# A two-layer encoder in float32: 36 of 44 gate-and-up tiles by seven half-size products in place of eight, the feed-forward in five groups

## The chip, the cores and the metric

The kernel runs on one core of one Trainium2 chip. The metric is the device time of one execution in microseconds (us), the median of several. The engines are named as in the profile: PE is TensorE (PEld its weight loads), DVE is VectorE, ACT is ScalarE, POOL is GpSimd, SP is SyncE, which here only issues transfers. A matmul of TensorE writes to PSUM (eight banks); DVE and ACT read from there.

## The reference, cut to what matters

Two layers on x of 512 positions by 1024 features, all in float32. Each layer mixes by attention and then runs a gated feed-forward, which is what the change is about:

```python
for l in range(DEPTH):                       # DEPTH = 2
    h = rms_norm(x, attn_norm_g[l])
    ...                                      # projections, retention, differential attention
    x = x + jnp.concatenate([ret, da], axis=-1) @ w_out[l]
    h = rms_norm(x, ffn_norm_g[l])
    x = x + (jax.nn.silu(h @ w_gate[l]) * (h @ w_up[l])) @ w_down[l]
```

w_gate and w_up are 1024 by 2816, w_down is 2816 by 1024.

## The kernel before, in words

**Three products for one.** A float32 matmul at full precision is made of three in the format fp32r: every operand is split into hi (the value rounded to fp32r) and lo (what is left), and a product is hi·hi + hi·lo + lo·hi (mm3, L184 to L187). For a piece of weights of 128 by 1024, SP loads it into a tile raw (three of these), ACT casts it to hi (L177), and DVE subtracts to get lo (L178); of hi and of lo there are three tiles each (NHL = 3). So ACT and DVE have to have prepared a piece before TensorE gets to it, and its hi and lo tiles come free only when TensorE has used them.

**The layout.** Features lie on the 128 partitions, positions (512) on the free axis. h2 is a list of eight pairs (hi, lo), one for each 128 features; the row factor 1/rms (rstd2) is put on after the product.

**The feed-forward (FFN, L637 onwards).** The 2816 inner features are 22 tiles of 128, in three groups: 8, 8 and 6. For each tile (loop over ff) come two chunks of weights, gate and up. Each is 8 times mm3, so 24 matmuls with 512 columns into a PSUM bank; DVE multiplies by rstd2 (L655, L658), ACT does SiLU on the gate (L105), DVE multiplies the two (L659), and split makes hi and lo of the result (L203 on ACT, L204 on DVE). After a group come the eight output pieces of "down" (loop over m): each loads 128 by 128·(tiles of the group) of w_down, runs mm3 over the group's tiles into one bank, and DVE adds it to x (residual, L614). After the last group of layer 0 the residual also makes the next layer's norm and split; after that of layer 1 it is stored.

**What sets the order.** The program text is one stream; the framework's scheduler then lays the instructions of each engine in an order of its own from planned times, and puts in semaphore waits. On the chip each engine runs its list strictly in that order, so an instruction that waits holds up all behind it on its engine. PSUM has two banks each of the tags acc, sc and o (any_bank goes round them) and two of aux.

**The start.** PE runs nine matmuls on a zeroed tile (L117) while the first data come. ACT issues the loads of the parameters (prm) and then of the first piece of x; SP issues the first weights in half pieces and the other pieces of x in turn.

Of the kernel before, what the change touches and what calls it, by code (L numbers as in the profile page):

```python
# [22 lines left out]
FT = DFF // P  # L23
EPS = 1e-6
C = 256
# [17 lines left out]

PRM_AG, PRM_FG, PRM_RG, PRM_QG, PRM_KG, PRM_DG = 0, 16, 32, 34, 36, 38
# [9 lines left out]
def encoder_kernel(ctx: ExitStack, tc: tile.TileContext, xT, wfirst, wsingle, wvv, wout, wgu, wdn, prm, lam, cst, outT):  # L54
    nc = tc.nc
# [3 lines left out]
    wpool = ctx.enter_context(tc.tile_pool(name="wpool", bufs=3))  # L59
# [25 lines left out]
    def any_bank():  # L85
        turn[0] += 1
        return (acc_bank, sc_bank, out_bank)[turn[0] % 3]()

    consts = {}

    def f32(ap):
        return ap.bitcast(F32)
# [15 lines left out]


    prm_sb = cpool.tile([P, PRM_N], F32, name="prm_sb")  # L110
    nc.scalar.dma_start(prm_sb, prm)

    warm = big("warm", F32R)
    nc.vector.memset(f32(warm), 0.0)
    warm_bank = aux_bank()
    for i in range(NWARM):
        nc.tensor.matmul(warm_bank, warm[:, :P], warm, start=True, stop=True)  # L117
# [44 lines left out]
    def load_chunk(src, n=1024, pieces=1):  # L162
# [2 lines left out]
            load_piece(new, src, i)  # L165
        return new

    def split_chunk(raw, n, pieces, first=False):
        hi = wpool.tile([P, 1024], F32R, tag="hi", name=nm("hi"), bufs=NHL)
        lo = wpool.tile([P, 1024], F32R, tag="lo", name=nm("lo"), bufs=NHL)  # L170
        q = n // pieces
        for i in range(pieces):
            s = slice(i * q, (i + 1) * q)
            if first and i == 0:
                nc.vector.tensor_copy(hi[:, s], raw[:, s])
            else:
                nc.scalar.copy(hi[:, s], raw[:, s])  # L177
            nc.vector.tensor_tensor(lo[:, s], raw[:, s], f32(hi[:, s]), op=ALU.subtract)  # L178
        return hi, lo

    def chunk(*a, **kw):
        return split_chunk(*load_chunk(*a, **kw))

    def mm3(out, L, R, start, stop):  # L184
        nc.tensor.matmul(out, L[0], R[0], start=start, stop=False)  # L185
        nc.tensor.matmul(out, L[0], R[1], start=False, stop=False)  # L186
        nc.tensor.matmul(out, L[1], R[0], start=False, stop=stop)  # L187

    def cut(pair, *idx):
        return tuple(t[idx] for t in pair)  # L190

    def split_scaled(src, col, tag, bufs):

        hi = big("hi", F32R, tag, bufs)
        lo = big("lo", F32R, tag, bufs)
        nc.scalar.activation(hi, src, AF.Copy, scale=col)  # L196
        nc.vector.scalar_tensor_tensor(lo, src, col, f32(hi), op0=ALU.mult, op1=ALU.subtract)
        return hi, lo

    def split(src, tag, bufs):  # L200
        hi = big("hi", F32R, tag, bufs)
        lo = big("lo", F32R, tag, bufs)
        nc.scalar.copy(hi, src)  # L203
        nc.vector.tensor_tensor(lo, src, f32(hi), op=ALU.subtract)  # L204
        return hi, lo
# [84 lines left out]
    def layer(l, n1, h, x_src, first_raw):  # L290
# [322 lines left out]
        def residual(m, xt, ps, n, hn, g):  # L613
            nc.vector.tensor_tensor(xt, xt, ps, op=ALU.add)  # L614
            if n is not None:
                n.add(xt)
                hn.append(split_scaled(xt, prm_sb[:, g + m : g + m + 1], "h", 16))

        def project_out(half, get, *then):
            parts = mix[4:] if half == 0 else mix[:4]  # L620
# [20 lines left out]

        rstd2 = n2.rows()
        n3, h3 = Norm(), []
        for a0, a1 in FFN:
            act = []
            for ff in range(a0, a1):
                pgu = []
                for gu in range(2):
                    w = [t.rearrange("p (k f) -> p k f", f=P) for t in chunk(wgu[l, ff, gu])]
                    ps = any_bank()  # L650
                    for kt in range(KT):
                        mm3(ps, cut(w, slice(None), kt), h2[kt], kt == 0, kt == KT - 1)
                    pgu.append(ps)
                g = big("g")
                nc.vector.tensor_tensor(g, pgu[0], rstd2, op=ALU.mult)  # L655
                func(g, g, AF.Silu)
                u = big("u")
                nc.vector.tensor_tensor(u, pgu[1], rstd2, op=ALU.mult)  # L658
                nc.vector.tensor_tensor(u, g, u, op=ALU.mult)  # L659
                act.append(split(u, *(("rn", 4) if ff - a0 < 2 and a0 else ("mix", NMIX))))  # L660
            last = a1 == FT
            for m in range(KT):
                w = chunk(wdn[l, m][:, a0 * P : a1 * P], (a1 - a0) * P)
                ps = any_bank()
# [12 lines left out]
    for kt in range(KT):  # L677
        if kt % 2 == 0:
            raws.append(new_chunk(1024, 2))
        load_piece(raws[-1], wfirst[0, kt // 2], kt % 2)  # L680
        xt = load_x(xT, kt, nc.scalar if kt == 0 else None)
        h.append(split_scaled(xt, prm_sb[:, PRM_AG + kt : PRM_AG + kt + 1], "h", 16))
        n.add(xt)
    for l in range(DEPTH):
        if l:
# [19 lines left out]
def _layout(inputs):  # L705
    import numpy as np

    f = {k: np.asarray(v) for k, v in inputs.items()}
    a = {}
    a["xT"] = f["x"].reshape(T, D).T.reshape(KT, P, T)  # L710
    w = f["w_in"].reshape(DEPTH, KT, P, 3584).transpose(0, 2, 1, 3)
    cols = {"rq": 0, "rk": 512, "rv": 1024, "rg": 1536, "dq": 2048, "dk": 2560, "dv": 3072}

    def sel(n, f, width):
        return w[:, :, :, cols[n] + f : cols[n] + f + width]

# [12 lines left out]
    g = f["w_gate"].reshape(DEPTH, KT, P, FT, P).transpose(0, 3, 2, 1, 4).reshape(DEPTH, FT, 1, P, 1024)  # L729
    u = f["w_up"].reshape(DEPTH, KT, P, FT, P).transpose(0, 3, 2, 1, 4).reshape(DEPTH, FT, 1, P, 1024)  # L730
    a["wgu"] = np.concatenate([g, u], 2)
# [43 lines left out]
```

## Time and profile before

| | |
|---|---|
| median of 3 runs | 1273.31 us (1273.26 to 1275.16) |
| the profiled execution | 1275.36 us |
| its span, first to last instruction | 1273.5 us |
| PE busy | 1264.8 us, 6201 matmuls |
| DVE / ACT busy | 769.7 / 569.8 us |
| read from HBM | 114.87 MB |
| granted TensorE clock, mean | 1.00 |

The profile gives an engine's busy time and, in groups by line and shape, the mean duration of an instruction. Matmuls overlap: one with 512 columns lasts 0.39 us, yet the next one starts long before it ends. So the time that a matmul costs is the distance from start to start, which the timeline shows, and not its duration. The same holds to a lesser degree for DVE and ACT.

### The profile page before, as it was taken

How to read it: one execution, taken by the hardware profiler on the slowest of the kernel's cores; microseconds unless marked ns; L12 is line 12 of the kernel's file. 1: busy time of each engine (PE TensorE's matmuls, PEld its weight loads, DVE VectorE, ACT ScalarE, POOL GpSimd, SP SyncE). 2: the span in 40 equal slices, each digit the busy share in tenths (PEclk: the TensorE clock that was granted, in tenths of full speed). 3: DMA queues.
4: the chain of work that ended last, by engine and by line, in shares of the span. 5: the costliest groups of instructions: out<-in, count | busy, mean ns of one | idle time of the engine just before them, and what ended most of it. 6: DMA issues, size and time to landing. Idle time of an engine off the chain costs nothing.

```text
span 1273.5 us, 15689 instructions
## 1 busy us (share of the span) xinstructions
PE 1264.8 (99%) x6201; PEld 1056.9 (83%) x6201; DVE 769.7 (60%) x1193; ACT 569.8 (45%) x886; POOL 17.3 (1%) x38
## 2 busy tenths in 40 slices
PE   9999999999999999999999999999999999999998
PEld 7888998778888888888888889987788888888887
DVE  6899759966443444344648997697754434443443
ACT  6777747554321322123438785564542223322221
POOL 1000000000000000000000000000000000000000
PEclk9999999999999999999999999999999999999999
DMA  7222224113333332322432122141233333333222
GB/s 266 83 67 67 67 66 133 58 60 114 90 97 96 99 99 84 115 91 81 159 117 83 50 84 66 51 149 51 66 116 99 99 91 93 98 99 99 99 76 91
DMA packets 36793, 120.07 MB, mean 94 GB/s; under 512 B 4208, under 2 KB 4208, under 8 KB 36592
## 3 DMA queue, kind: packets, MB, share of 16 engines
q1 hardware_dynamic: 36432, 118.77, 29.3%
q8 instruction: 48, 0.79, 0.2%
q10 hardware_dynamic: 288, 0.31, 0.1%
q14 instruction: 25, 0.20, 0.1%
HBM read 114.87 MB, written 4.19 MB: 93 GB/s over the span
## 4 chain that ended last, share of the span: by engine, by line
PE 97%; DVE 1%; ACT 1%; DMA 0%; issue 0%; SPq 0%
PE acc L185 15%; PE acc L186 15%; PE acc L187 15%; PE o L185 8%; PE o L187 8%; PE o L186 8%; PE sc L185 7%; PE sc L187 7%; PE sc L186 7%; PE sc L380 2%; PE o L481 1%; PE sc L465 1%; PE aux L396 1%; PE aux L137 1%; PE aux L136 1%; PE aux L441 1%
## 5 line engine op out<-in xcount | busy, mean ns | idle before, releaser
L177 ACT CAST hi<-raw 128x1024 fp32r<-128x1024 f32 (+2 forms) x211 | 215.0, 1021 | 511.8 <-issue 153.7
L185 PE MATMUL acc<-hi,hi 128*128 128x512 f32 (+1 forms) x914 | 337.6, 370 | 1.0 <-ACT hi L196 0.7
L186 PE MATMUL acc<-lo,hi 128*128 128x512 f32 (+1 forms) x914 | 337.8, 370 | 0.0
L187 PE MATMUL acc<-hi,lo 128*128 128x512 f32 (+1 forms) x914 | 337.1, 369 | 0.0
L178 DVE TENSOR_TENSOR lo<-raw,hi 128x1024 fp32r<-128x1024 f32 (+2 forms) x212 | 250.2, 1182 | 43.5 <-ACT hi L177 43.1
L185 PEld LDWEIGHTS acc<-hi,hi 128*128 128x128 f32 x914 | 172.4, 189 | 31.9 <-ACT hi L196 1.4
L186 PEld LDWEIGHTS acc<-lo,hi 128*128 128x128 f32 x914 | 172.6, 189 | 28.9 <-issue 1.2
L187 PEld LDWEIGHTS acc<-hi,lo 128*128 128x128 f32 x914 | 172.6, 189 | 28.0
L185 PE MATMUL o<-hi,hi 128*128 128x512 f32 (+1 forms) x438 | 163.9, 374 | 0.0
L186 PE MATMUL o<-lo,hi 128*128 128x512 f32 (+1 forms) x438 | 163.7, 374 | 0.0
L187 PE MATMUL o<-hi,lo 128*128 128x512 f32 (+1 forms) x438 | 163.6, 374 | 0.0
L185 PE MATMUL sc<-hi,hi 128*128 128x512 f32 x408 | 158.7, 391 | 0.3 <-ACT hi L177 0.3
L186 PE MATMUL sc<-lo,hi 128*128 128x512 f32 x408 | 159.0, 390 | 0.0
L187 PE MATMUL sc<-hi,lo 128*128 128x512 f32 x408 | 158.9, 389 | 0.0
L185 PEld LDWEIGHTS o<-hi,hi 128*128 128x128 f32 x438 | 82.4, 188 | 15.6 <-DVE sq L496 0.7
L186 PEld LDWEIGHTS o<-lo,hi 128*128 128x128 f32 x438 | 82.4, 188 | 14.8
L187 PEld LDWEIGHTS o<-hi,lo 128*128 128x128 f32 x438 | 82.4, 188 | 14.6
L185 PEld LDWEIGHTS sc<-hi,hi 128*128 128x128 f32 x408 | 76.9, 188 | 17.4 <-issue 0.8
L186 PEld LDWEIGHTS sc<-lo,hi 128*128 128x128 f32 x408 | 76.8, 188 | 16.1
L187 PEld LDWEIGHTS sc<-hi,lo 128*128 128x128 f32 x408 | 76.7, 188 | 15.9
L105 ACT ACTIVATE sc<-sc,mx 128x512 f32<-128x512 f32 x64 | 46.0, 720 | 16.8 <-DVE mx L384 16.4
L614 DVE TENSOR_TENSOR x<-x,acc 128x512 f32<-128x512 f32 x36 | 24.5, 684 | 37.9 <-PE acc L187 37.8
(137 smaller groups left out, 1288.3 us busy)
## 6 DMA issues: line engine op xcount, KB each, us to landing
raw<-in_wgu SPq DMA_DIRECT2D x88, 512.0 KB, 3.5
raw<-in_wsingle SPq DMA_DIRECT2D x32, 512.0 KB, 3.5
raw<-in_wdn SPq DMA_DIRECT2D x32, 512.0 KB, 3.5
raw<-in_wvv SPq DMA_DIRECT2D x16, 512.0 KB, 3.5
raw<-in_wout SPq DMA_DIRECT2D x16, 512.0 KB, 3.6
raw<-in_wdn SPq DMA_DIRECT2D x16, 384.0 KB, 3.2
x<-in_xT SPq DMA_DIRECT2D x15, 256.0 KB, 4.3
raw<-in_wfirst SPq DMA_DIRECT2D x8, 256.0 KB, 5.4
```

What stands on the lines that cost most here:

```text
L105: i = nc.scalar.activation(out, src, f, **kw).ins
L136: nc.tensor.matmul(ps, w, hi, start=True, stop=False)
L137: nc.tensor.matmul(ps, w, lo, start=False, stop=True)
L177: nc.scalar.copy(hi[:, s], raw[:, s])
L178: nc.vector.tensor_tensor(lo[:, s], raw[:, s], f32(hi[:, s]), op=ALU.subtract)
L185: nc.tensor.matmul(out, L[0], R[0], start=start, stop=False)
L186: nc.tensor.matmul(out, L[0], R[1], start=False, stop=False)
L187: nc.tensor.matmul(out, L[1], R[0], start=False, stop=stop)
L380: nc.tensor.matmul(ps, q[m][:, t], k[m][part], start=part == 0, stop=part == 1)
L396: nc.tensor.transpose(tp[:, j * P : (j + 1) * P], a[:, j * P : (j + 1) * P], ident)
L441: nc.tensor.matmul(kv[:, d * P : (d + 1) * P], kw[:, jj * P : (jj + 1) * P], v[pr // 2][jj][:, e], start=j == 0, stop=j == 1)
L614: nc.vector.tensor_tensor(xt, xt, ps, op=ALU.add)
```

## The change

**Seven products (Strassen's scheme in Winograd's form).** For the inner tiles 4 to 21 of each layer, gate and up are no longer 2 times 24 matmuls with 512 columns. The four blocks of the weights are (gate, first 512 features), (gate, last 512), (up, first), (up, last); the four blocks of the moving side are halves of the features by halves of the positions (256 columns). Seven products of the half-size blocks replace eight. Each is 4 steps of 128 features times three matmuls with 256 columns, so a tile takes 84 matmuls with 256 columns (L740). The first four tiles of a layer (PLAIN) stay as they were; while they run, the function combine makes, from x, the sums and differences of the moving blocks and their hi and lo, once for a layer.

**What a tile (a "unit", function seven) needs beside the matmuls.** Four additions of 512 columns on the weights on DVE (L725 to L728, the tiles s31 and s24); hi and lo of s31, of the whole gate chunk a (it holds gate-first and up-last), of half of the up chunk b, and of s24 (L714 on ACT, L715 on DVE). s31 and a use the three hi and lo tiles of the weights (parts, tags hi and lo). Three products add up in the same bank pa (tag acc) after each other: g1·b11, then s2·t2, s3·t3 and u2·t4 on top; between these the sum so far is read out, by DVE (L748) and by ACT (copies at L751 and L754). Two more products share bank pc (tag o), one has pb (tag sc).

**The rest.** Down runs in five groups (4 plain tiles, then 5, 5, 4 and 4), so w_down comes in smaller pieces and there are 40 residual additions in a layer in place of 24. The last output piece of all is done in two halves of 256 columns, each stored at once. At the start, PE runs eight zero matmuls with 512 columns and eight with 128 in place of nine with 512; the first piece of x is loaded ahead of the parameters; the first hi of x is put ahead of the second weight cast on ACT. The tiles of the moving side are allocated in pairs under the tag h.

The diff, cut to its core:

```diff
-FFN = [(0, 8), (8, 16), (16, FT)]
+FFN = [(0, 4), (4, 9), (9, 14), (14, 18), (18, FT)]
+PLAIN = FFN[0][1]
...
-NWARM = 9
+NWARM, NWARM_SHORT = 8, 8
...
-    for i in range(NWARM):
-        nc.tensor.matmul(warm_bank, warm[:, :P], warm, start=True, stop=True)
+    for n in [T] * NWARM + [P] * NWARM_SHORT:
+        nc.tensor.matmul(warm_bank[:, :n], warm[:, :P], warm[:, :n], start=True, stop=True)
...
+    x_first = load_x(xT, 0, nc.scalar)
+    nc.scalar.dma_start(prm_sb, prm)
...
+    def parts():
+        return tuple(wpool.tile([P, 1024], F32R, tag=t, name=nm(t), bufs=NHL) for t in ("hi", "lo"))
...
+        def split_in(raw, hi, lo, n=1024):
+            nc.scalar.copy(hi, raw[:, :n])
+            nc.vector.tensor_tensor(lo, raw[:, :n], f32(hi), op=ALU.subtract)
+            return [(hi[:, i * T : (i + 1) * T], lo[:, i * T : (i + 1) * T]) for i in range(n // T)]
...
+        def seven(ff, act, tag, bufs):
+            a, b = load_chunk(wgu[l, ff, 0])[0], load_chunk(wgu[l, ff, 1])[0]
+            s31, s24 = (tpool.tile([P, 1024], F32, tag="ah", name=nm("s"), bufs=NAH) for _ in range(2))
+            u1 = b[:, T:]
+            nc.vector.tensor_tensor(s31[:, :T], u1, a[:, :T], op=ALU.subtract)
+            nc.vector.tensor_tensor(s31[:, T:], u1, a[:, T:], op=ALU.subtract)
+            nc.vector.tensor_tensor(s24[:, :T], a[:, :T], s31[:, T:], op=ALU.subtract)
+            nc.vector.tensor_tensor(s24[:, T:], b[:, :T], s24[:, :T], op=ALU.subtract)
+            s3, s1 = split_in(s31, *parts())
+            g1, u2 = split_in(a, *parts())
+            (g2,) = split_in(b, big("g2h", F32R), big("g2l", F32R), T)
+            s2, s4 = split_in(s24, wide(), wide())
+            pa, pb, pc = (bank() for bank in (acc_bank, sc_bank, out_bank))
...
+            g, u, v = big("g"), big("u"), big("v")
+            product(pc, s1, "t1", True)
+            yield
+            product(pa, g1, "b11", True)
+            product(pb, g2, "b21", True)
+            nc.scalar.copy(v[:, H1], pb[:, :C])
+            nc.vector.tensor_tensor(g[:, H1], pa[:, :C], v[:, H1], op=ALU.add)
+            yield
+            product(pa, s2, "t2", False)
+            nc.scalar.copy(v[:, H2], pa[:, :C])
+            yield
+            product(pa, s3, "t3", False)
+            nc.scalar.copy(u[:, H1], pa[:, :C])
+            nc.vector.tensor_tensor(u[:, H2], pc[:, :C], u[:, H1], op=ALU.add)
+            yield
+            product(pa, u2, "t4", False)
+            product(pc, s4, "b22", False)
+            nc.vector.tensor_tensor(g[:, H2], pc[:, :C], v[:, H2], op=ALU.add)
+            func(g, g, AF.Silu)
+            nc.vector.tensor_tensor(u[:, H1], pa[:, :C], g[:, H1], op=ALU.mult)
+            nc.vector.tensor_tensor(u[:, H2], u[:, H2], g[:, H2], op=ALU.mult)
+            act.append(split(u, tag, bufs))
```

**How the order moves, PE.** In the middle of the FFN, PE went from one chunk of weights to the next like this before (here from an up to a gate or down product; sc_4296 and o_4337 are two PSUM banks, the second name behind the arrow is the weight tile):

```order
L186 MATMUL sc_4296<-lo_2977,hi_4292 128x512
L187 MATMUL sc_4296<-hi_2976,lo_4293 128x512
L185 MATMUL o_4337<-hi_2804,hi_4333 128x512 [waits Activation_49]
L186 MATMUL o_4337<-lo_2805,hi_4333 128x512
L187 MATMUL o_4337<-hi_2804,lo_4334 128x512 [waits DVE_49]
```

The new bank waits for the cast of its own weights alone. Now the place in the third and fourth unit of a group where the s3 product of one unit ends (acc_3787 with the weights hi_3771 and lo_3772, which came from s31), the first two matmuls of the next unit's g1 stand (acc_3915 with hi_3903, which came from that unit's chunk a), and the first unit's u2 product begins (weights hi_3775):

```order
L740 MATMUL acc_3787<-hi_3386,hi_3771 128x256
L740 MATMUL acc_3787<-lo_3387,hi_3771 128x256
L740 MATMUL acc_3787<-hi_3386,lo_3772 128x256
L740 MATMUL acc_3915<-bh_3068,hi_3903 128x256 [waits DVE_49,Activation_49]
L740 MATMUL acc_3915<-bl_3069,hi_3903 128x256
L740 MATMUL acc_3787<-hi_3083,hi_3775 128x256 [waits Activation_49]
```

The two matmuls on acc_3915 wait for the cast of hi_3903, and the next on acc_3787 for the ACT copy that reads the bank out; both stand right behind the s3 product.

**How the order moves, ACT.** Before, in the FFN, ACT's list holds for a tile two casts of weights, a SiLU and a cast of the result:

```order
L105 ACTIVATE g_3889<-g_3889 128x512 [waits DVE_49]
L177 CAST hi_3973<-raw_3971 128x1024 [waits DMAHW7_49,PE_49,Activation_49]
L203 CAST hi_3895<-u_3892 128x512 [waits DVE_49]
L177 CAST hi_4004<-raw_4002 128x1024 [waits DMAHW0_49,PE_49,Activation_49]
L105 ACTIVATE g_3961<-g_3961 128x512 [waits DVE_49]
```

Now, at the same unit border as above:

```order
L751 COPY v_3792<-acc_3787 128x256 [waits PE_49]
L215 CAST h_3873<-u_3663 128x512 [waits DVE_49]
L714 CAST s_3911<-s_3894 128x1024
L714 CAST hi_3903<-raw_3889 128x1024 [waits DMAHW1_49,PE_49,Activation_49]
L754 COPY u_3791<-acc_3787 128x256 [waits PE_49,Activation_49]
L747 COPY v_3920<-sc_3916 128x256
L714 CAST hi_4027<-s_4021 128x1024 [waits DVE_49,PE_49,Activation_49]
L714 CAST g2h_4035<-raw_4019 128x512 [waits DMAHW4_49]
L106 ACTIVATE g_3790<-g_3790 128x512 [waits DVE_49]
```

The cast of hi_3903 has a wait for PE in it, and the copy of the bank (L754) stands behind it in ACT's list. The PE instruction for which that cast waits is the eleventh of the twelve matmuls of the s3 product, the last that reads hi_3771: with three hi tiles and two taken by each unit, a unit's chunk a gets the tile that the unit before used for s31.

More of the change, by code (lines that the diff above doesn't have):

```diff
@@ L176, in split_chunk @@
             else:
-                nc.scalar.copy(hi[:, s], raw[:, s])
+                c = nc.scalar.copy(hi[:, s], raw[:, s])
+                if first:
+                    tc.add_manual_dep(c.ins, first_part[0], order, reason="first part of x")
             nc.vector.tensor_tensor(lo[:, s], raw[:, s], f32(hi[:, s]), op=ALU.subtract)
@@ L200, in split @@
     def split(src, tag, bufs):
-        hi = big("hi", F32R, tag, bufs)
-        lo = big("lo", F32R, tag, bufs)
+        hi, lo = pair() if tag == "h" else [big(n, F32R, tag, bufs) for n in ("hi", "lo")]
         nc.scalar.copy(hi, src)
@@ L616, in residual @@
                 n.add(xt)
-                hn.append(split_scaled(xt, prm_sb[:, g + m : g + m + 1], "h", 16))
+                hn.append(split_scaled(xt, prm_sb[:, g + m : g + m + 1]))
         def project_out(half, get, *then):
@@ L643, in layer, with gate_up @@
         n3, h3 = Norm(), []
-        for a0, a1 in FFN:
[L645 to L661, printed above, removed]
+        def gate_up(ff, tag, bufs):
+            pgu = []
+            for gu in range(2):
+                w = [t.rearrange("p (k f) -> p k f", f=P) for t in chunk(wgu[l, ff, gu])]
+                ps = any_bank()
+                for kt in range(KT):
+                    mm3(ps, cut(w, slice(None), kt), h2[kt], kt == 0, kt == KT - 1)
+                pgu.append(ps)
+            g = big("g")
+            nc.vector.tensor_tensor(g, pgu[0], rstd2, op=ALU.mult)
+            func(g, g, AF.Silu)
+            u = big("u")
+            nc.vector.tensor_tensor(u, pgu[1], rstd2, op=ALU.mult)
+            nc.vector.tensor_tensor(u, g, u, op=ALU.mult)
+            return split(u, tag, bufs)
@@ new lines, in layer, with part256, combine @@
+        H1, H2 = slice(0, C), slice(C, T)
+        comb = []
+        def part256(src):
+            hi = tpool.tile([P, 256], F32R, tag="dv", name=nm("bh"), bufs=16)
+            lo = tpool.tile([P, 256], F32R, tag="dv", name=nm("bl"), bufs=16)
+            nc.scalar.copy(hi, src)
+            nc.vector.tensor_tensor(lo, src, f32(hi), op=ALU.subtract)
+            return hi, lo
+        def combine(i):
+            b1, b2 = big("b"), big("b")
+            for t, kt in ((b1, i), (b2, i + 4)):
+                nc.vector.scalar_tensor_tensor(t, x[kt], prm_sb[:, PRM_FG + 8 * l + kt : PRM_FG + 8 * l + kt + 1], rstd2, op0=ALU.mult, op1=ALU.mult)
+            ta, tb = big("ta"), big("tb")
+            nc.vector.tensor_tensor(ta[:, H1], b1[:, H2], b1[:, H1], op=ALU.subtract)
+            nc.vector.tensor_tensor(ta[:, H2], b2[:, H2], ta[:, H1], op=ALU.add)
+            nc.vector.tensor_tensor(tb[:, H1], b2[:, H2], b1[:, H2], op=ALU.add)
+            nc.vector.tensor_tensor(tb[:, H2], b2[:, H1], ta[:, H2], op=ALU.subtract)
+            b11, b21 = part256(b1[:, H1]), part256(b2[:, H1])
+            b22 = big("b22", F32R, *[("w", NW), ("qk", NQK), ("mix", NMIX), ("mix", NMIX)][i])
+            nc.scalar.copy(b22[:, H1], b2[:, H2])
+            nc.vector.tensor_tensor(b22[:, H2], b2[:, H2], f32(b22[:, H1]), op=ALU.subtract)
+            ta = split(ta, "mix", NMIX)
+            tb = split(tb, *(("mix", NMIX) if i else ("qk", NQK)))
+            comb.append(
+                dict(
+                    b11=b11, b21=b21, b22=(b22[:, H1], b22[:, H2]),
+                    t1=cut(ta, slice(None), H1), t2=cut(ta, slice(None), H2), t3=cut(tb, slice(None), H1), t4=cut(tb, slice(None), H2),
+                )
+            )
@@ new lines, in layer @@
+        for a0, a1 in FFN:
+            act, last = [], a1 == FT
+            if a1 <= PLAIN:
+                for ff in range(a0, a1):
+                    act.append(gate_up(ff, *(("mix", NMIX) if ff < 2 else ("rn", 4))))
+                    combine(ff)
+            else:
+                units = []
+                for ff in range(a0, a1):
+                    tag = ("h", 8) if not last else ("mix", NMIX) if ff < a0 + 2 else ("rn", 4)
+                    units.append(seven(ff, act, *tag))
+                next(units[0])
+                next(units[0])
+                for i, unit in enumerate(units):
+                    then = units[i + 1] if i + 1 < len(units) else iter([0, 0])
+                    next(unit)
+                    next(then)
+                    next(unit)
+                    next(then)
+                    next(unit, None)
```

42 lines of the change are left out of this document (31 added, 11 removed).

## The prediction

> **What bounds the kernel now.** I read the page first: the span, the busy times, the clock, and the chain that ended last, with its shares by engine.
>
> ```profile
> span 1273.5 us, 15689 instructions
> PE 1264.8 (99%) x6201; PEld 1056.9 (83%) x6201; DVE 769.7 (60%) x1193; ACT 569.8 (45%) x886; POOL 17.3 (1%) x38
> PEclk9999999999999999999999999999999999999999
> PE 97%; DVE 1%; ACT 1%; DMA 0%; issue 0%; SPq 0%
> ```
>
> TensorE is busy 99% of the span at full clock, and the chain runs along it. Next came the list of waits, for PE its two largest entries (total us, count, longest), and the busy times in a stretch inside the first FFN (PE, PEld, DVE, ACT, POOL, then clock, DMA share, GB/s).
>
> ```profile
> PE sc L380 <- DVE mx L384: 1.9, 5, 0.5
> PE acc L185 <- ACT hi L196: 0.7, 1, 0.7
> ```
>
> ```profile
> 340.00:640.00 300.00, 300.00 (x1325) 248.43 (x1324) 136.12 (x162) 88.24 (x107) 3.58 (x7) 1.00 0.33 103
> ```
>
> In the FFN, PE never stops; DVE is busy 45% there and ACT 29%. Hence time there is the number of matmuls times their spacing, and anything new that PE has to wait for is paid in full. Spacings come from the timeline (start, duration, instruction). The first two rows are 16 intervals apart, the other two 26.
>
> ```profile
> 421.35 0.39 PE L187 MATMUL sc<-hi,lo 128*128 128x512 f32 x1
> ...
> 424.98 0.39 PE L185 MATMUL o<-hi,hi 128*128 128x512 f32 x1
> ```
>
> ```profile
> 45.75 0.28 PE L185 MATMUL o<-hi,hi 128*128 128x256 f32 x1
> ...
> 48.87 0.28 PE L187 MATMUL o<-hi,lo 128*128 128x256 f32 x1
> ```
>
> That is 3.63/16 = 0.227 us for 512 columns and 3.12/26 = 0.120 for 256: half the width costs 53%, not 50%.
>
> **The matmuls.** A tile had 48 x 0.2269 = 10.89 us and gets 84 x 0.120 = 10.08. So 0.81 us a tile, 36 tiles: **-29.1 us**, Seven for eight at an equal cost per column would be 1.36 a tile; the 6.6 ns by which 0.120 exceeds half of 0.2269 take 0.55 of it, 20 us over all tiles. I take the measured spacing, since its 26 intervals have the same three matmuls with weight loads between them. What falls away on DVE and ACT lay beside PE's work and brings nothing, and the transfers (DMA a third busy above) stay hidden: down is only read in other pieces.
>
> **The hand-overs.** The second PE extract shows the price of the scheme: when the s3 product ends, PE's next matmuls want a weight tile whose cast could not begin before the eleventh matmul of that product. I price one such hand-over by three pieces. First, from a matmul's start to the start of the ACT instruction it releases, for 256 and for 512 columns:
>
> ```profile
> 139.85 0.28 PE L187 MATMUL o<-ah,dvl 128*128 128x256 f32 x1
> 140.17 0.60 ACT L141 ACTIVATE sq<-o 128x512 f32<-128x512 f32 x1 [0.72 <-PE o L187]
> ...
> 404.81 0.39 PE L186 MATMUL sc<-lo,hi 128*128 128x512 f32 x1
> 405.23 1.05 ACT L177 CAST hi<-raw 128x1024 fp32r<-128x1024 f32 x1 [4.38 <-PE sc L186]
> ```
>
> 0.32 and 0.42 us. Second, the released work (groups by shape: busy total, mean ns, then idle before).
>
> ```profile
> L177 ACT CAST hi<-raw 128x1024 fp32r<-128x1024 f32 x188 | 197.6, 1052 | 469.4 <-issue 138.5 <-PE acc L186 127.8 <-PE sc L186 110.1
> L177 ACT CAST hi<-raw 128x768 fp32r<-128x768 f32 x16 | 13.2, 837 | 41.8 <-issue 15.2 <-PE sc L186 11.8 <-PE acc L186 9.7
> L203 ACT CAST hi<-u 128x512 fp32r<-128x512 f32 x44 | 27.5, 625 | 33.6 <-DVE u L659 33.6
> L399 ACT CAST ah<-aux 128x512 fp32r<-128x512 f32 x32 | 18.5, 579 | 13.4 <-PE aux L396 13.4
> L178 DVE TENSOR_TENSOR lo<-raw,hi 128x1024 fp32r<-128x1024 f32 x188 | 229.6, 1222 | 43.5 <-ACT hi L177 43.1
> L204 DVE TENSOR_TENSOR lo<-u,hi 128x512 fp32r<-128x512 f32 x44 | 30.2, 686 | 2.9 <-ACT hi L203 2.8
> ```
>
> A cast of 1024 is 1.05. No row has 640 columns: between 0.625 and 0.837, I take 0.73. A PSUM copy of 256 columns: 0.579 for 512, less 0.21 (837 - 625) per 256, gives 0.37. A DVE instruction of 256: 0.686 less half of 1222 - 686, gives 0.42. Third, PE's restart. Here DVE releases a weight load, and two matmuls follow:
>
> ```profile
> 68.48 0.08 DVE L384 DVE_READ_ACCUMULATOR2_ANT mx<- 128x1 f32 x1
> 68.61 0.19 PEld L380 LDWEIGHTS sc<-khi,q 128*128 128x128 f32 x1 [0.76 <-DVE mx L384]
> 68.62 0.50 PE L380 MATMUL sc<-khi,q 128*128 128x512 f32 x1 [0.34 <-DVE mx L384]
> 68.95 0.40 PE L380 MATMUL sc<-klo,q 128*128 128x512 f32 x1
> ```
>
> The load starts 0.05 after DVE's end, and the second matmul comes 0.33 after the first in place of 0.227: 0.16 in all. (Bounds: 0.05, if the first matmul's delay is hidden, and 0.16.)
>
> Counted over the order of both layers, with the PE work that lies between release and need:
> a) 16 unit borders as in the extract, with one matmul (0.12) between. The next start would be 0.24 after the eleventh matmul; now it is 0.32 + 1.05 + 0.16 = 1.53. 1.29 each, **20.6 us**. The copy L754, behind that cast on ACT, ends about 1.7 after the eleventh matmul (0.32 + 1.05 + 0.37); the two g1 matmuls carry PE to 1.77, so it adds nothing here.
> b) 12 borders where ten other matmuls lie between (1.44 to the next start): 0.09 each, **1.1**.
> c) 10 copies L751 between s2 and s3, with two matmuls as cover (0.36): 0.32 + 0.37 + 0.16 = 0.85, so 0.49 each, **4.9**.
> d) 4 additions L748 with no cover, in the first units of two groups: 0.32 + 0.42 + 0.16 = 0.90 against 0.12, 0.78 each, **3.1**.
> e) The eight group ends. The second down piece's cast finds no free tile in time: 3.0 in all with the prices above and 0.1 to 0.8 of cover. The last unit's chain (L759, SiLU, L761, L762, cast, subtraction) is 0.32 + 0.42 + 0.05 + 0.62 + 0.05 + 0.33 + 0.42 + 0.05 + 0.62 + 0.16 = 3.04, against twelve matmuls of 512 columns (2.84 with the next start) in four groups and nine (2.16) in four: 0.8 + 3.5. Three casts with 1.1 of cover: 1.5. **8.8**.
>
> Together **+38.5**: a tile with wait a) costs 11.37 us, more than the 10.89 it had. Bounds: if restart is 0.05, 45 waits are 0.11 shorter, -5; if the scheduler's cover at group ends holds twice as well, -4.4.
>
> **VectorE's room.** Its new work (four additions of 512, two of lo more, five of 256 on PSUM) is hidden if independent instructions overlap. Pairs from the timeline, the first independent, the second dependent:
>
> ```profile
> 87.37 0.68 DVE L204 TENSOR_TENSOR lo<-sq,hi 128x512 fp32r<-128x512 f32 x1
> 87.97 0.68 DVE L353 SCALAR_TENSOR_TENSOR sq<-aux,sq 128x512 f32<-128x512 f32 x1
> ```
>
> ```profile
> 59.77 0.68 DVE L353 SCALAR_TENSOR_TENSOR sq<-aux,sq 128x512 f32<-128x512 f32 x1
> 60.49 0.69 DVE L354 SCALAR_TENSOR_TENSOR u<-sq,u 128x512 f32<-128x512 f32 x1
> ```
>
> 0.60 against 0.72. The tightest ring: chunk b's raw tile is loaded again only when g2l of the unit before is done.
>
> ```profile
> raw<-in_wgu SPq DMA_DIRECT2D x88, 512.0 KB, 3.5
> ```
>
> 3.5 for the load, 0.1, then ten DVE instructions up to the next g2l; with 0.60 for 512 columns, 1.13 for 1024 and 0.33 for 256 they take 7.1. Together 10.7, under the 11.37 of a unit: hidden, by 0.6. In the plain tiles the sums of combine, with what these tiles have anyway, come to 10 us of DVE at most by the same spacings, in 10.89 of PE: hidden too, and if DVE were slower each of eight tiles would be late by the excess.
>
> **Start and end.** Matmuls, casts and the first loads of before:
>
> ```profile
> 1.46 4.21 PE L117 MATMUL aux<-warm 128*128 128x512 f32 x9 [1.46 <-DVE eps_sb L151]
> 5.07 0.62 ACT L177 CAST hi<-raw 128x512 fp32r<-128x512 f32 x1 [0.66 <-DMA raw<-in_wfirst]
> 5.59 0.72 ACT L196 ACTIVATE hi<-x,prm_sb 128x512 fp32r<-128x512 f32 x1
> 6.36 1.22 PE L185 MATMUL acc<-hi,hi 128*128 128x512 f32 x2 [0.70 <-ACT hi L196]
> ...
> 9.09 0.63 PE L186 MATMUL acc<-lo,hi 128*128 128x512 f32 x1
> 9.51 0.63 PE L187 MATMUL acc<-hi,lo 128*128 128x512 f32 x1
> ...
> 10.68 0.40 PE L186 MATMUL sc<-lo,hi 128*128 128x512 f32 x1
> ```
>
> PE stands still from 5.67 to 6.36 and then runs at half speed (0.42 spacing) until 10.68. The hi of x, ahead of the second cast, comes up to 0.5 earlier. If the standstill is what puts off full speed, the short zero matmuls that now fill it save up to half of the 4.3 us at half speed, 2.2. I take the first whole and two thirds of the second, **-1.9**; bounds 0 (x lands no earlier, the clock rises as late) and -2.7. At the end, the last addition:
>
> ```profile
> 1269.01 0.39 PE L187 MATMUL o<-hi,lo 128*128 128x512 f32 x1
> 1269.44 0.69 DVE L614 TENSOR_TENSOR x<-x,o 128x512 f32<-128x512 f32 x1 [3.39 <-PE o L187]
> ```
>
> Half of it is now done earlier: 0.686 - 0.42, **-0.3** (0 to -0.6).
>
> **The sum.** -29.1 + 38.5 - 1.9 - 0.3 = +7.2 us. The profiled execution took 1275.36, 2.05 above the median of 1273.31; on the median the sum gives **1280.5 us**.
>
> **Rivals.** *R0, no wait shows* (the casts are through when PE comes): 1273.3 - 29.1 - 2.2 = 1242. Against it: a cast takes 1.05 and one matmul of cover 0.12. Chance 0.08.
>
> *R1, cheaper hand-overs* (restart 0.05, group ends half): 38.5 - 9.4 = 29.1 us of waits, so 1271. They and the gains are even at 31.3. For it: one kind of wait, five in number, is all that shows a restart. Chance 0.22.
>
> *R2, a half-width matmul costs half*: without the 6.6 ns the sum is 20 lower, 1261. Against it stands the 0.120. Chance 0.04. [...]
>
> *R3, VectorE becomes the bound*: if its instructions are spaced as the dependent pair is (0.72 for 0.60), the ten take 8.3, the ring 11.9, 0.5 over a unit; 16 units lose 8 us. L748 stands in the steady units right behind the subtraction for the next s31; by the 0.60 spacing it ends just when PE needs it, so it would be 0.13 late in some twenty units, another 2 to 3. Together 1290 to 1292: slower in any case. It decides once the spacings are 9% above the independent ones (7.8 us for the ten). For it: two of the four additions depend on the one before them. Against it: unlike neighbours show 0.60. Chance 0.15. [...]
>
> That the products do not become fewer is excluded: the order has 1728 matmuls less of 512 columns and 3024 more of 256.
>
> **How the numbers follow.** The forecast case, 1274.5 to 1287, has 0.51. A difference of 0.2%, 2.5 us, is about what a measurement of this kernel can tell. Faster: R0, R2 and 0.13 of R1, 0.25. Within 0.2%: 0.09 of R1 and 0.09 of the forecast, 0.18. Slower: 0.42 of the forecast and R3, 0.57. The range, 1266 to 1293, leaves out R0, R2 and the far ends of R1 and R3.
>
> **What would show it.** Right: in the FFN, PE waiting for ACT's cast about 1.2 us, 16 times, first in the list of waits; spacing 0.120 in the products; L751 and L748 next. [...]

## The result, and the profile after

The changed kernel takes 1314.24 us (median of four runs, 1313.12 to 1316.28) against 1273.51 for the kernel before: a ratio of 1.032, 95% interval 1.0307 to 1.0332. It is 40.7 us slower. Slower was forecast, but by 7.2 us and within 1293. The first rows of the page and the head of PE's list of waits (total us, count, longest):

```profile
span 1313.1 us, 19158 instructions
PE 1263.8 (96%) x7516; PEld 1100.5 (84%) x7516; DVE 972.4 (74%) x1634; ACT 683.4 (52%) x1138; POOL 17.3 (1%) x38
```

```profile
PE acc L740 <- ACT hi L714: 17.0, 16, 1.1
PE acc L740 <- DVE g L748: 7.4, 4, 2.3
PE acc L740 <- DVE lo L715: 3.3, 6, 1.1
PE o L740 <- DVE lo L715: 2.2, 4, 0.8
PE acc L740 <- ACT v L751: 2.0, 9, 0.2
```

The 16 waits for the cast of chunk a stand first, as forecast. The rows below it hold the news: four long waits for L748, and ten for lo tiles (L715) that the forecast did not have at all. A recorded wait begins when the matmul before has ended, so a wait costs about 0.16 more than its row says (a matmul lasts 0.28 and is spaced 0.12), and the matmul behind it starts another 0.10 late. I therefore worked the cost out from the start times of all matmuls in the timeline: the distance to the next start, less 0.2269 or 0.120, put down to the wait at that place. Before, both FFNs together have less than 0.5 us of such excess. After, they have 70.5:

| | forecast, us | measured, us |
|---|---|---|
| matmuls, 36 tiles | -29.1 | -29.1 |
| a) 16 casts of chunk a | 20.6 | 21.8 |
| b) waits over just in time, no row of their own | 1.1 | 8.9 |
| c) copies L751 | 4.9 | 4.4 |
| d) additions L748 | 3.1 | 8.3 |
| e) ends of the Strassen groups | 8.8 | 7.1 |
| end of the plain group | none | 6.3 |
| lo tiles late (L715) | none | 8.1 |
| stretches at half clock | none | 4.5 |
| smaller rests | | 1.1 |
| start and end | -2.2 | -0.6 |

The sum is -29.1 + 70.5 - 0.6 = 40.8, beside 40.7 measured. That it fits to 0.1 is luck, since the four runs of the changed kernel spread over 3.2 us. The last line is what start_end shows below. The matmuls are right to the tenth: apart from waits, the 3024 are spaced 0.120.

**Term a in the timeline**, at the place that the order's second extract shows (PE, then ACT):

```profile
371.33 0.28 PE L740 MATMUL acc<-lo,hi 128*128 128x256 f32 x1
371.45 0.28 PE L740 MATMUL acc<-hi,lo 128*128 128x256 f32 x1
372.79 0.39 PE L740 MATMUL acc<-bh,hi 128*128 128x256 f32 x1 [1.06 <-ACT hi L714]
373.01 0.28 PE L740 MATMUL acc<-bl,hi 128*128 128x256 f32 x1
```

```profile
371.70 1.04 ACT L714 CAST hi<-raw 128x1024 fp32r<-128x1024 f32 x1 [1.80 <-issue]
372.65 0.37 ACT L754 COPY u<-acc 128x256 f32<-128x256 f32 x1
```

The eleventh matmul of s3 starts at 371.33 and the cast at 371.70, 0.37 later (0.32 was taken). PE's start goes from 371.57 to 372.79, 1.22, and the second matmul follows after 0.22 in place of 0.12. With the restart that is 1.32; 1.29 was forecast. Over the 16, with a few hundredths at the next matmul (373.13 to 373.29), it is 1.36 each.

**What is late on VectorE.** Of DVE's list of waits, one row is new; below it DVE's instructions where PE waits longest for L748.

```profile
DVE s L725 <- DMA raw<-in_wgu: 28.9, 28, 2.2
```

```profile
350.18 1.21 DVE L715 TENSOR_TENSOR s<-s,s 128x1024 fp32r<-128x1024 f32 x1
352.35 0.69 DVE L725 TENSOR_TENSOR s<-raw,raw 128x512 f32<-128x512 f32 x1 [0.96 <-DMA raw<-in_wgu]
352.95 0.69 DVE L726 TENSOR_TENSOR s<-raw,raw 128x512 f32<-128x512 f32 x1
353.56 0.42 DVE L748 TENSOR_TENSOR g<-acc,v 128x256 f32<-128x256 f32 x1
```

```profile
351.47 0.28 PE L740 MATMUL acc<-bh,lo 128*128 128x256 f32 x1
354.03 0.58 PE L740 MATMUL acc<-hi,s 128*128 128x256 f32 x1 [2.28 <-DVE g L748]
354.41 0.41 PE L740 MATMUL acc<-lo,s 128*128 128x256 f32 x1
```

DVE had nothing to do from 351.39 to 352.35: the first addition on the next unit's weights stood at the head of its list and waited for their load. L748, for which PE stood still, was behind it, and then behind two additions (1.2 us) as well. The spacing of 0.60 holds (352.35, 352.95, 353.56). The same place makes lo of chunk a late in later units:

```profile
457.09 0.69 DVE L725 TENSOR_TENSOR s<-raw,raw 128x512 f32<-128x512 f32 x1 [0.64 <-DMA raw<-in_wgu]
457.70 0.68 DVE L726 TENSOR_TENSOR s<-raw,raw 128x512 f32<-128x512 f32 x1
458.30 1.22 DVE L715 TENSOR_TENSOR lo<-raw,hi 128x1024 fp32r<-128x1024 f32 x1
```

At the end of the plain group, combine's sums and their lo tiles stand between the last tile's result u and its lo, though the hi that this lo needs was done at 328.94 (ACT's cast, 328.32 and 0.62):

```profile
327.60 0.69 DVE L670 TENSOR_TENSOR u<-g,u 128x512 f32<-128x512 f32 x1
328.20 0.42 DVE L696 TENSOR_TENSOR ta<-b 128x256 f32<-128x256 f32 x1
...
330.48 0.42 DVE L697 TENSOR_TENSOR ta<-b,ta 128x256 f32<-128x256 f32 x1
330.81 0.69 DVE L216 TENSOR_TENSOR lo<-u,hi 128x512 fp32r<-128x512 f32 x1
```

**Half clock.** After the long wait the matmuls follow at 0.21, not 0.12 (busy time and count of PE, PEld, DVE, ACT and POOL, then the granted clock, DMA share and GB/s):

```profile
354.00:357.20 3.20, 3.17 (x15) 3.17 (x16) 2.91 (x4) 0.98 (x2) 0.00 (x0) 0.50 0.19 29
357.40:361.00 3.60, 3.60 (x32) 3.60 (x32) 2.43 (x3) 1.68 (x2) 0.00 (x0) 1.00 0.29 113
```

### The profile page after: what moved, and what is told of

It reads as the page before. It is cut to its first block, busy times and chain, and to the rows that moved or that the text cites. A ratio compares the mean times of both kernels' runs of the same rounds, so it can differ in the third digit from the quotient of the medians.

```text
span 1313.1 us, 19158 instructions
## 1 busy us (share of the span) xinstructions
PE 1263.8 (96%) x7516; PEld 1100.5 (84%) x7516; DVE 972.4 (74%) x1634; ACT 683.4 (52%) x1138; POOL 17.3 (1%) x38
## 3 DMA queue, kind: packets, MB, share of 16 engines
q1 hardware_dynamic: 41040, 118.64, 29.1%
## 4 chain that ended last, share of the span: by engine, by line
PE 38%; DVE 6%; DMA 3%; ACT 2%; issue 2%; DVEq 0%; ACTq 0%; SPq 0%
PE acc L740 6%; PE acc L198 5%; PE acc L199 5%; PE acc L200 5%; DMA raw<-in_wgu 3%; PE o L740 3%; PE o L198 2%; PE o L199 2%; PE o L200 2%; PE sc L198 2%; PE sc L199 1%; PE sc L200 1%; PE sc L392 1%; PE sc L740 1%; DVE lo L715 1%
## 5 line engine op out<-in xcount | busy, mean ns | idle before, releaser
L191 DVE TENSOR_TENSOR lo<-raw,hi 128x1024 fp32r<-128x1024 f32 (+2 forms) x172 | 166.2, 972 | 69.9 <-ACT hi L187 69.2
L198 PE MATMUL acc<-h,hi 128*128 128x512 f32 x411 | 161.8, 395 | 0.7 <-DVE u L761 0.4
L199 PE MATMUL acc<-h,hi 128*128 128x512 f32 x411 | 161.0, 392 | 0.0
L200 PE MATMUL acc<-h,lo 128*128 128x512 f32 x411 | 160.7, 392 | 0.0
L198 PEld LDWEIGHTS acc<-h,hi 128*128 128x128 f32 x411 | 77.1, 188 | 19.8 <-ACT hi L187 2.4
L200 PEld LDWEIGHTS acc<-h,lo 128*128 128x128 f32 x411 | 77.2, 188 | 16.0
L199 PEld LDWEIGHTS acc<-h,hi 128*128 128x128 f32 x411 | 77.2, 188 | 15.5 <-DVE h L216 0.4
L740 PE MATMUL acc<-hi,hi 128*128 128x256 f32 x288 | 83.3, 289 | 2.1 <-ACT v L751 2.0
L740 PE MATMUL acc<-lo,hi 128*128 128x256 f32 x288 | 81.3, 282 | 0.0
L740 PE MATMUL acc<-hi,lo 128*128 128x256 f32 x288 | 81.2, 282 | 0.0
L740 PE MATMUL acc<-hi,s 128*128 128x256 f32 x288 | 61.2, 295 | 7.4 <-DVE g L748 7.4
L714 ACT CAST hi<-s 128x1024 fp32r<-128x1024 f32 x36 | 37.8, 1051 | 55.3 <-DVE s L726 34.2
L715 DVE TENSOR_TENSOR lo<-raw,hi 128x1024 fp32r<-128x1024 f32 x36 | 43.9, 1220 | 27.8 <-ACT hi L714 27.8
L714 ACT CAST hi<-raw 128x1024 fp32r<-128x1024 f32 x36 | 37.7, 1048 | 51.5 <-issue 29.5
L740 PE MATMUL acc<-bh,hi 128*128 128x256 f32 x144 | 43.6, 303 | 17.0 <-ACT hi L714 17.0
L740 PEld LDWEIGHTS acc<-hi,hi 128*128 128x128 f32 x288 | 54.6, 190 | 5.1 <-ACT v L751 4.6
L198 PE MATMUL sc<-h,hi 128*128 128x512 f32 x147 | 57.7, 396 | 0.6 <-ACT h L215 0.6
L740 PE MATMUL o<-b,s 128*128 128x256 f32 x432 | 57.6, 283 | 0.0
L199 PE MATMUL sc<-h,hi 128*128 128x512 f32 x147 | 57.4, 391 | 0.0
```

The costliest lines, as they stand in the source:

```text
L714: nc.scalar.copy(hi, raw[:, :n])
L715: nc.vector.tensor_tensor(lo, raw[:, :n], f32(hi), op=ALU.subtract)
L740: nc.tensor.matmul(ps[:, :C], L[x1], R[x2], start=start and k + i == 0, stop=k == 3 and i == 2, skip_group_check=True)
```

## The experiments

Theory 1: two kinds of hand-over cost the time. One is the ring of three hi tiles. The other is a list in strict order, above all VectorE's, in which work that is not urgent or has to wait for a load stands ahead of work that TensorE is waiting for. Theory 2, the rival: VectorE, now 74% busy, has too much to do, and the order of its list does not matter. The kernel before, on the same chip as the first four, took 1273.56 us. The ratios stand with their 95% intervals; they are not simply the quotients of the medians. Line numbers move with the edits: the matmuls of the seven products are L740, L744 or L748, and the text names the other lines as in the changed kernel.

**dve_order: the additions behind L748.** An edge that only orders:

```diff
-            nc.vector.tensor_tensor(s31[:, :T], u1, a[:, :T], op=ALU.subtract)
-            nc.vector.tensor_tensor(s31[:, T:], u1, a[:, T:], op=ALU.subtract)
+            for h in (slice(0, T), slice(T, 2 * T)):
+                d = nc.vector.tensor_tensor(s31[:, h], u1, a[:, h], op=ALU.subtract)
+                for n in ahead:
+                    tc.add_manual_dep(d.ins, n, order, reason="behind the unit before")
...
-            nc.vector.tensor_tensor(g[:, H1], pa[:, :C], v[:, H1], op=ALU.add)
+            ahead[:] = [nc.vector.tensor_tensor(g[:, H1], pa[:, :C], v[:, H1], op=ALU.add).ins.name]
```

> The changed kernel, with one order edge: on VectorE the two additions on a unit's fresh weights stand behind the addition that reads the unit before out of PSUM (before, they stood ahead of it and waited there for the weights' load). TensorE's list comes out with ten matmuls, not one, behind the cast of chunk a. Theory 1 (two hand-overs: the ring of three hi tiles, and a VectorE list blocked by additions that wait for loads): the 21.8 us behind casts of chunk a fall to 3, the waits for L748 from 8.3 to about 3.6, those for the lo tiles (L715) from 8.1 to under 3, the half-clock stretches in the Strassen units go: 1268 to 1276 us. Theory 2 (VectorE, 74% busy, simply has too much to do): the waits for VectorE stay at 16 us or more, 1290 or more.

Measured: 1281.57 us, ratio 1.0059 (1.0044 to 1.0074). The largest rows of PE's waits and DVE's wait for loads:

```profile
PE acc L744 <- DVE g L752: 6.0, 8, 0.9
PE sc L392 <- DVE mx L396: 1.9, 5, 0.5
PE sc L198 <- ACT hi L215: 1.7, 2, 1.0
```

```profile
DVE s L728 <- DMA raw<-in_wgu: 10.3, 8, 2.1
```

32.7 us come back from one edge, though the instructions are the same and DVE is about as busy as before (966.6 us). The excess in the FFNs falls from 70.5 to 36.2. Theory 2 is refuted: DVE does the same work in 34 us less, and the waits for L748 and L715, restarts included, fall from 16.4 to 8.1 us. But the gain is not all VectorE's, since the scheduler, with this edge, also lays ten matmuls behind the cast of chunk a. Worked out from the start times as above, half of the 34.3 us lies there: about 17 at the unit borders (the 21.8 go, and the waits that are over just in time grow from some 9 to 13, as all 28 borders are now of this kind), 8.1 for L715, 3.9 for the copies L751, 3.0 for the half clock (one stretch of three is left, at the end of a plain group), and small rests. The number lies outside both expectations: L748 (here line 752) no longer waits behind loads, but its bare price of 0.75 to 1.08 falls due in all eight first units (8.1 us), not in four; and theory 1 had 3 where those borders now cost more than 4.

**swap_hi: the ring by itself.**

```diff
-            s3, s1 = split_in(s31, *parts())
             g1, u2 = split_in(a, *parts())
+            s3, s1 = split_in(s31, *parts())
```

> The changed kernel with two lines exchanged: hi and lo of chunk a are taken from the ring before those of s31. Only 8 of the 16 bare hand-overs are left in TensorE's list. Theory 1: 8 times 1.36 us less behind the casts of chunk a, and where L748 is no longer without cover its 8.3 us and the half clock go too: 1290 to 1304 us. Theory 2 (VectorE too full): the waits move from the casts to VectorE, 1308 or more.

Measured: 1285.17 us, ratio 1.0087 (1.0072 to 1.0102), 5 us better than theory 1's range. The largest rows:

```profile
PE o L740 <- ACT hi L714: 11.1, 12, 1.2
PE o L740 <- DVE lo L715: 1.8, 4, 0.5
PE acc L740 <- DVE g L748: 1.2, 5, 0.3
```

```profile
DVE s L725 <- DMA raw<-in_wgu: 29.7, 31, 2.2
```

The waits for the cast are now those of s31, twelve (14.6 us with restarts) and not eight; L748 costs 2.5 with restarts. In the Strassen units the half clock is gone; one stretch is left, at the end of the first plain group (331.83 to 335.25). DVE waits for loads as long as before, yet PE's waits for L748 and L715 fall from 12.9 to 3.4 us in the list. So DVE's wait for a load is not in itself a cost to PE. That it depends on what is queued behind it fits this, but PE's order changed too, and this run does not part the two.

**noload: no load to wait for.** Only the first unit of a group loads gate and up weights; the others use them again, so most of the gate and up products are not those of the reference.

```diff
-            a, b = load_chunk(wgu[l, ff, 0])[0], load_chunk(wgu[l, ff, 1])[0]
+            if not once:
+                once.extend(load_chunk(wgu[l, ff, gu])[0] for gu in range(2))
+            a, b = once
```

> The changed kernel, in which all units of a group use the weights that the first unit loaded (the other gate and up weights are left out, the arithmetic stays): no addition waits for a load. TensorE's list has 28 bare hand-overs of chunk a here, in place of 16. Theory 1: behind these 28 times 1.36, 38 us (16 more); the waits for L748 fall from 8.3 to 3.6 or less and those for L715 from 8.1 to under 2, the half clock goes: 1310 to 1320 us, and VectorE shows no wait for a load in the units but the first of a group. Theory 2: the waits for L748 and L715 stay at 14 us or more, 1326 or more.

Measured: 1319.43 us, ratio 1.0354 (1.0339 to 1.037), inside theory 1's range. But its reasons hold only in part:

```profile
PE acc L744 <- ACT hi L714: 30.1, 28, 1.1
PE acc L744 <- DVE g L752: 5.8, 8, 1.0
PE o L744 <- DVE lo L715: 3.0, 6, 1.1
```

The 28 bare casts cost 38.3 us, 1.37 each: term a goes with their count. The half clock is gone from the Strassen units; one stretch is left at the end of the first plain group. The waits for L748 and L715 together are 13.5 us in place of 16.4, where theory 1 had under 6 and theory 2 had 14 or more: on this count the run lies nearer to theory 2, and only the order edge above refutes that. These waits largely outlive the loads. Additions that need not wait themselves still stand ahead, and the first unit of each group still loads (DVE waits eight times, 10.5 us). Since eight first units wait for L748 here and not four, the run does not say how much of the 16.4 was the loads.

**five: five groups in the kernel before.**

```diff
-FFN = [(0, 8), (8, 16), (16, FT)]
+FFN = [(0, 4), (4, 9), (9, 14), (14, 18), (18, FT)]
```

> The kernel before with five groups in place of three, all tiles plain. Theory 1: the group ends cost what they do (about 13 us) because of the chain of the last Strassen unit and the casts behind it, not because there are more of them: 1273 to 1277 us. Rival: smaller down pieces and more group ends cost by themselves, 1280 to 1288 us.

Measured: 1273.86 us, ratio 1.0003 (0.9993 to 1.0012): the smaller pieces of down and the two more group ends cost nothing that these runs can tell. What a group's end costs comes with the Strassen units and with combine.

**start_end: the edits of start and end alone**, on three groups of plain tiles. (The weights are taken in the arrangement made for the Strassen tiles, so gate and up are mixed; the instructions are those of plain tiles.)

```diff
-FFN = [(0, 4), (4, 9), (9, 14), (14, 18), (18, FT)]
+FFN = [(0, 8), (8, 16), (16, FT)]
...
+            for ff in range(a0, a1):
+                act.append(gate_up(ff, *(("rn", 4) if ff - a0 < 2 and a0 else ("mix", NMIX))))
```

> The kernel before with the edits of start and end alone (short zero matmuls, x first, its hi ahead of the second cast, last output piece in halves; the pairs under one tag too), three groups, all tiles plain. Theory: the 2 us by which the first FFN of the changed kernel begins earlier come from these edits, and 0.3 at the end: 1271.0 to 1271.8 us, below the kernel before. Rival: the earlier begin comes from elsewhere in the changed order, 1273 to 1274 us.

Measured: 1272.94 us; the kernel before on that chip had 1275.04, ratio 0.9991 (0.9982 to 1.0). Neither expectation: the kernel before has two start positions, 2 us apart. Its runs lie at 1273.2 to 1274.0 or at 1275.0 to 1275.7 (11 and 14 runs); those of start_end at 1272.6 to 1273.3, but for one at 1275.21. Within the earlier position the edits bring 0.6. The profiles show the two, with the same start code, for start_end and for the changed kernel:

```profile
7.00:10.60 3.60, 3.60 (x10) 2.73 (x10) 3.60 (x8) 3.60 (x7) 0.00 (x0) 1.00 1.05 404
```

```profile
7.00:10.60 3.60, 3.60 (x18) 2.93 (x17) 3.60 (x8) 3.60 (x7) 0.00 (x0) 1.00 1.05 390
```

In 3.6 us PE does 10 matmuls in the one and 18 in the other. The clock column is a mean over what the trace has on record, and the first record, with 1.00, begins only at 10.73 us in the one, at 5.73 in the other. The start code does not decide it: with the code of before, the profile of before has its first record at 10.52 and that of five at 4.69. Whether the edits make the earlier one likelier (10 of 11 runs against 11 of 25) stays open; plain_first, with the same start, had the late one in its profile (the first multiplication of its first FFN, L666, starts at 301.92, that of the changed kernel at 299.76).

**plain_first: combine's last sums behind the last plain tile**, on top of dve_order.

```diff
+                if i == PLAIN - 1:
+                    tc.add_manual_dep(d.ins, done[0], order, reason="behind the last plain tile")
```

(d is the first operation of combine, done[0] the subtraction that makes the tile's lo.)

> The kernel with the order edge on the additions (dve_order), and a second edge: the sums of combine for the last of the four pairs stand behind the chain of the last plain tile on VectorE. Theory 1 (lists blocked by work that is not urgent): the waits of the first group's down pieces for the last tile's hi and lo, about 3.2 us in each layer, fall to 1 or less: 1276 to 1279 us. Theory 2 (VectorE's amount of work): the same time as with the first edge, 1281 to 1282 us, and the first Strassen unit later by what the tile gains.

Measured: 1276.59 us, ratio 1.0022 (1.0012 to 1.0032): some 5 us less from one more edge, as theory 1 had it (3.2 less in the excess of the two profiles). DVE's work is the same, and the two waits of 1.6 us for lo of the last tile (L216) have left PE's list. Part of it has only moved, as theory 2 had foreseen: 5.5 us of waits at the plain groups' ends and the last stretch at half clock (1.6) are gone, but 3.7 us of waits for lo tiles of the first Strassen units have come in, above all for g2l:

```profile
PE sc L748 <- DVE g2l L719: 1.3, 3, 0.5
```

**best1: cover for the first unit**, on top of plain_first.

```diff
+            if first:
+                product(pb, g2, "b21", True)
+                product(pc, s1, "t1", True, range(2, 4), product(pa, g1, "b11", True))
```

(The last argument is the matmul behind which the second half of s1 has to stand.)

> As plain_first, and in the first unit of a group TensorE's order is g2, half of s1, g1, the other half of s1, then s2, so that six matmuls lie between g1 and the product that needs its sum read out. Theory 1: the eight waits for that addition, 8.1 us together, fall to 2 or less: 1270 to 1273.5 us, level with or below the kernel before. Rival: what is late there is hi and lo of the first unit's weights, and the wait moves to them: 1276 us or more.

Measured: 1271.70 us beside 1275.04, ratio 0.9979 (0.997 to 0.9989). Against the 16 runs of before beside the next experiment, 1271.67 and 1274.36, ratio 0.9981 (0.9972 to 0.9991). This version is faster than both kernels, by 0.2% than the one before. Some of that can be the mix of start positions; against the runs of before in the earlier position (1273.2 to 1274.0) it is 0.1%. The waits for the addition L748 (here line 764) have left the list. Of the waits below, 4.5 us with restarts, those for g2l were there in plain_first; those for lo of chunk a have grown from 0.6 to 2.0, so the rival is right for a part:

```profile
PE acc L748 <- DVE lo L719: 2.0, 2, 1.0
PE sc L392 <- DVE mx L396: 1.9, 5, 0.5
PE sc L748 <- DVE g2l L719: 1.2, 3, 0.5
```

> The kernel best1 once more, unchanged, beside best2 on the same chip: 1270 to 1273 us, 0.1 to 0.3% below the kernel before.

(That is the second number above.)

**best2: more cover for the cast**, on top of best1. The edge:

```diff
-                product(pa, g1, "b11", True)
+                product(pa, g1, "b11", True, behind=u2_end[0])
```

(u2_end holds the last matmul of u2; the loop over the units now also goes on with u2 before the next unit's g1.)

> As best1, and between two units TensorE's order is s3, ten of s1, u2, then g1 whole, so that the cast of the next unit's chunk a has 22 matmuls of cover in place of 10. Theory 1: the 28 unit borders, which cost 0.16 us each in best1 (the wait is over just when TensorE comes, and the matmul behind it starts 0.10 late), cost nothing: 4 us less, 1266 to 1269 us. Rival: the copy of the bank that u2 needs, behind that cast on ScalarE, is then late: 1271 or more.

Measured: 1277.78 us, ratio 1.0028 (1.0016 to 1.0039): 6 us slower than best1, and the rival is right. PE's largest wait, and ACT and PE at a border:

```profile
PE acc L748 <- ACT u L770: 3.2, 10, 0.4
```

```profile
366.69 1.05 ACT L718 CAST hi<-raw 128x1024 fp32r<-128x1024 f32 x1 [2.14 <-issue]
367.64 0.37 ACT L770 COPY u<-acc 128x256 f32<-128x256 f32 x1
```

```profile
367.64 0.28 PE L748 MATMUL o<-hi,lo 128*128 128x256 f32 x1
368.06 0.39 PE L748 MATMUL acc<-hi,hi 128*128 128x256 f32 x1
```

The copy that u2 needs stands behind that cast on ACT and ends at 368.01; u2 now comes first on PE and waits 0.3. In best1 the two matmuls of g1 stood there as cover. An order is right only for all lists together.

## Why the prediction was wrong

Right were the direction, the saving of the matmuls, the mechanism and price of a (1.36 with restart, 1.29 forecast; 1.37 where there were 28), term c, and roughly the ends of the Strassen groups (7.1 for 8.8). The waits came to 70.5 us in place of 38.5. Of the 32 more, 19.6 are VectorE's (L748, L715 and the plain groups' ends), which the prediction had as hidden but for 3.1; 7.8 are term b and 4.5 the half clock. The steps that failed:

- **"Together 10.7, under the 11.37 of a unit: hidden, by 0.6."** The durations were right (0.60, 0.33, 1.13), but this compares DVE's throughput with a unit, and DVE could keep up. What counts is when one instruction comes through. The additions for the next unit stood ahead of L748 and of lo of chunk a, often waiting for a load (28 times). L715's 8.1 are gone in dve_order. The four waits for L748 cost 2.1 each; with the additions behind it, the same four cost 0.85, beside 0.78 forecast. So d's price was right for an empty list, and what stood ahead in DVE's list was left out.
- **"hidden too" of combine's sums.** The amount fits into the tiles' time, but the sums stood ahead of the last plain tile's own chain: 6.3 us at the ends of the two plain groups, where none was forecast. One edge (plain_first) takes most of that away, and 3.7 us come back in the units behind it.
- **Term b.** A cover of ten matmuls just suffices, and such a border costs 0.16, not 0.09 (in best1 the starts around g1's first two matmuls are 0.03, 0.10 and 0.03 late); and there are more of them than the 12: 111 gaps of 0.08 each.
- **Half clock.** It was not in the sum: 4.5 us in three stretches.
- **The start's -1.9.** Profiled run and median differ by the start position. I read the 2 us as something the edits would remove, and had already taken them off by going to the median. 0.6 was left of start and end. That the standstill puts off full speed is not shown: with the same start code, both 10 and 18 matmuls ran from 7.00 to 10.60.

The rival R3 named VectorE, and the time was above its 1290 to 1292. Its mechanism, additions spaced 0.72, did not occur. Its number was too low as well, since it priced a spacing and not a place.

What stays open: in dve_order, DVE's new order and the ten matmuls that the scheduler laid behind the cast came together, and no run here has the one without the other. The split by terms above (about 17 us at the borders, 8.1 for L715) is an account and not an experiment. More raw or hi tiles were not tried.

## What to carry to other kernels

An engine's share of busy time does not say whether its results come in time (VectorE was 74% busy here, and PE lost 19.6 us to it that were not forecast): for each instruction on which the bounding engine waits, read what stands ahead of it in its own engine's list, and ahead of all an instruction that waits for a load. A scheme that trades matmuls for many small hand-overs has to be priced by the count of hand-overs without cover (here 1.36 us each against 0.81 us saved in a tile). The same instructions gave 1314, 1282, 1277 and 1272 us under one to three ordering edges, so work that is not urgent should be put behind what is before a scheme is judged.

## What the runs showed of the hardware

- A stop of TensorE in mid-kernel can cost more than its length. After 2.28 us the granted clock was 0.50 for 3.41 us, which cost 1.5 more; the same followed after waits of 1.60 and 1.84 us, but not after others of 1.60, 1.56 and 1.70. So length alone does not decide. In the trace of the changed kernel, the times from one change of the granted clock on record to the next are 102, 1, 183, 1, 76, 1 and 19 times 3.413 us. Counted off in pieces of 3.413 us between these changes, the matmuls part the cases. From 5.73 us to the last matmul there are 382 such pieces. Half clock followed on the three in which PE stood still for 1.84 to 2.15 us, and on none of the others, where it stood still for 1.70 at most. The kernel before, whose record starts at 10.52 us, has 369 up to its last matmul, with a standstill of 0.64 at most, and its clock stays at 1.00. The three pieces of the changed kernel that were followed by half clock, and two that were not (length, then PE's busy time first):

```profile
350.48:353.89 3.41, 1.26 (x11) 1.06 (x9) 2.45 (x4) 1.15 (x3) 0.00 (x0) 1.00 0.70 270
978.53:981.94 3.41, 1.39 (x5) 0.87 (x6) 3.41 (x10) 1.09 (x3) 0.00 (x0) 1.00 0.01 4
1241.36:1244.77 3.41, 1.57 (x14) 1.36 (x13) 2.23 (x5) 1.53 (x3) 0.00 (x0) 1.00 0.55 191
1002.42:1005.84 3.42, 1.72 (x15) 1.52 (x14) 3.15 (x6) 1.67 (x2) 0.00 (x0) 1.00 0.29 116
330.00:333.41 3.41, 1.85 (x8) 1.34 (x8) 3.41 (x8) 2.16 (x4) 0.00 (x0) 1.00 0.00 0
```

So the wait of 1.60 that shared its piece with part of another of 0.65 (978.53) was followed by half clock, and the one in the piece at 330.00 was not. What the clock goes by is not shown.

- A wait that is over just when TensorE comes still costs about 0.10 us: the second matmul starts late (in best1 at 367.22, 0.22 from the first at 367.00, in place of 0.12).
- Two start positions, 2 us apart in the runs of the kernel before. In three of the eleven profiles the full clock is on record from 10.5 to 10.7 us on, in the other eight from somewhere between 4.7 and 7.6: read a profile's start before comparing it with a median.
